# Grouped output stores of an expert layer: 16 KB and 8 KB rows in place of 4 KB rows

## The chip, the cores and the metric

The kernel runs on one core of a Trainium2 chip. The metric is the device time of one execution in microseconds (us), as the median of several runs. The core has a matrix engine (PE), a vector engine (DVE), a scalar engine (ACT), GpSimd (POOL), a sync engine (SP), and sixteen DMA engines that move data between HBM and the on-chip memory SBUF. Matmul results land in PSUM, from where DVE or ACT copies them to SBUF ("eviction"). SBUF and PSUM have 128 partitions.

## The reference

Eight experts each apply a two-layer network to their own 256 tokens:

```python
# x [8, 256, 512], w1 [8, 512, 2048], w2 [8, 2048, 512], b1 [8, 2048], b2 [8, 512], all float32
h = np.matmul(x, w1) + b1[:, np.newaxis, :]
h = np.maximum(h, 0)
return (np.matmul(h, w2) + b2[:, np.newaxis, :]).astype(np.float32)   # [8, 256, 512]
```

The weights are 64 MB of float32 (67.1 million bytes), each used once. The result is 4 MB, 512 KB per expert.

## The kernel before

The weights are loaded by GpSimd's DMA queue, which casts them to fp16 on the way. One expert has 2 MB of w1 and 2 MB of w2 as fp16. The program runs in steps: step s does the first product of expert s and the second product of expert s - 3 (LAG = 3). Buffers for w1 and w2 are three each, so a load is issued when an older expert's matmuls have released a buffer.

```python
LAG = 3
LATE = range(E - 2)                       # experts 0 to 5
PARTS = {E - 2: ((0, 25, False), (25, 121, True), (121, 128, False))}
w1_pool = ctx.enter_context(tc.tile_pool(name="w1", bufs=3))
w2_pool = ctx.enter_context(tc.tile_pool(name="w2", bufs=3))
hT_pool = ctx.enter_context(tc.tile_pool(name="hT", bufs=LAG + 1))
out_pool = ctx.enter_context(tc.tile_pool(name="outp", bufs=E))
psum_h = ...bufs=3        # first product, [128, 256] float32 each
psum_o = ...bufs=2        # second product, two tiles of [128, 512] float32 each

def first_product(e):
    hT[e] = hT_pool.tile([P, nJ, T], fp16, tag="hT", name="hT")
    for j in range(nJ):                                   # 16 blocks of hidden units
        ph = psum_h.tile([P, T], fp32, tag="ph", name="ph")
        for kc in range(nKC):                             # 4 matmuls, ph = [hidden unit, token]
            ordered(nc.tensor.matmul(out=ph, lhsT=w1_sb[e]..., rhs=xT[e][:, kc, :], ...))
        nc.scalar.activation(out=hT[e][:, j, :], in_=ph, func=Relu, bias=b1T[...], scale=1.0)
        if j == nJ // 2 and e + 1 < E:
            transposes(e + 1)

def flush(e):
    dst, src = pending.pop(e)
    ordered(nc.gpsimd.dma_start(out=dst, in_=src))

def store(e, po):
    out_sb = out_pool.tile([P, nTB, H], fp32, tag="out", name="out")
    nc.vector.tensor_copy(out=out_sb[:, 0, :], in_=po[0])
    nc.scalar.copy(out=out_sb[:, 1, :], in_=po[1])
    dst = out[e].rearrange("(p tb) h -> p tb h", tb=nTB)  # a partition holds two result rows, 4 KB
    if e in LATE:
        pending[e] = (dst, out_sb)
        return
    for p0, p1, scalar in PARTS.get(e, ((0, P, False),)):
        (nc.scalar if scalar else nc.sync).dma_start(out=dst[p0:p1], in_=out_sb[p0:p1])

def second_product(e):
    ...   # bias row by a matmul with ones, then 16 matmuls for each half tb of the tokens:
    #       po[tb] += hT[e][:, j, tb * P : (tb + 1) * P] (transposed) x w2_sb[e][:, j, :]
    store(e, po)

# the ring holds loads and then the flushes; it is served from the front, in order
for e in LATE:
    ring.append((e + LAG + 1, flush, (e,)))
for s in range(E + LAG):
    while ring and ring[0][0] <= s:
        _, put, args = ring.pop(0)
        put(*args)
    if s < E:
        first_product(s)
    if s >= LAG:
        second_product(s - LAG)
```

Within each block of 256 tokens, the transposes put the tokens in such a column order that column tb * 128 + p is token 2p + tb. So partition p of the two result tiles holds rows 2p and 2p + 1, which lie side by side in HBM. The flushes of experts 0 to 5 stand in GpSimd's queue behind all loads. Expert 6 is stored in three pieces from SP and ACT, expert 7 in one from SP.

Of the kernel before, what the change touches and what calls it, by code (L numbers as in the profile page):

```python
# [10 lines left out]
def kernel(  # L11
# [9 lines left out]
    nc = tc.nc  # L21
    fp32 = mybir.dt.float32
    fp16 = mybir.dt.float16
    E, T, H = x.shape
    M = w1.shape[2]
    P = 128
    nTB = T // P
# [4 lines left out]
    LAG = 3  # L32

    LATE = range(E - 2)


    PARTS = {E - 2: ((0, 25, False), (25, 121, True), (121, 128, False))}
# [3 lines left out]
    def ordered(ins):  # L43
        return tc.keep_in_program_order(ins)
# [4 lines left out]
    x_pool = ctx.enter_context(tc.tile_pool(name="xp", bufs=1))  # L49
    xT_pool = ctx.enter_context(tc.tile_pool(name="xTp", bufs=2))  # L50
    hT_pool = ctx.enter_context(tc.tile_pool(name="hT", bufs=LAG + 1))
    out_pool = ctx.enter_context(tc.tile_pool(name="outp", bufs=E))
    psum_h = ctx.enter_context(tc.tile_pool(name="psum_h", bufs=3, space=bass.MemoryType.PSUM))
    psum_o = ctx.enter_context(tc.tile_pool(name="psum_o", bufs=2, space=bass.MemoryType.PSUM))

# [8 lines left out]
    w2_sb = [None] * E  # L64
    hT = [None] * E
    pending = {}

    def load_x(first, n):

        R = n * T // P  # L70
        t = x_pool.tile([P, R, H], fp16, tag=f"x{first}", name=f"x{first}")
        ordered(nc.gpsimd.dma_start(  # L72
            out=t, in_=x[first : first + n].rearrange("e (p r) h -> (e p) r h", r=R)
        ))
        for i in range(n):
            x16[first + i] = (t, i * (P // n), R)
# [13 lines left out]
    def transposes(e):  # L90


        t, p0, R = x16[e]
        n = R // nTB
        xT[e] = xT_pool.tile([P, nKC, T], fp16, tag="xT", name="xT")
        for g in range(T // R // B):
            src = t[p0 + B * g : p0 + B * (g + 1)]
            for b in range(nB):
                block = src[:, :, b * (H // nB) : (b + 1) * (H // nB)].rearrange(
                    "p (n tb) (i kc) -> p tb kc n i", tb=nTB, kc=nKC)  # L100
                out = xT[e][b * B : (b + 1) * B].rearrange(
                    "p kc (tb g i n) -> p tb g kc n i", tb=nTB, i=B, n=n)
                if n == 1:
                    nc.vector.transpose(out=out[:, :, g, :, 0, :], in_=block[:, :, :, 0, :])  # L104
                    continue
                for tb in range(nTB):
                    nc.vector.transpose(out=out[:, tb, g], in_=block[:, tb])  # L107

    def first_product(e):
        hT[e] = hT_pool.tile([P, nJ, T], fp16, tag="hT", name="hT")  # L110
        for j in range(nJ):
            bias_at = j * B + e * nB + nB - 1
            ph = psum_h.tile([P, T], fp32, tag="ph", name="ph")
            for kc in range(nKC):
                ordered(nc.tensor.matmul(  # L115
                    out=ph,
                    lhsT=w1_sb[e][:, kc, :].rearrange("p (q j) -> p q j", j=nJ)[:, :, j],
                    rhs=xT[e][:, kc, :],
                    start=(kc == 0),
                    stop=(kc == nKC - 1),  # L120
                ))
            nc.scalar.activation(  # L122
                out=hT[e][:, j, :],
                in_=ph,
                func=mybir.ActivationFunctionType.Relu,
                bias=b1T[:, bias_at : bias_at + 1],
                scale=1.0,
            )
            if j == nJ // 2 and e + 1 < E:
                transposes(e + 1)  # L130

    def flush(e):
        dst, src = pending.pop(e)
        ordered(nc.gpsimd.dma_start(out=dst, in_=src))  # L134

    def store(e, po):
        out_sb = out_pool.tile([P, nTB, H], fp32, tag="out", name="out")
        nc.vector.tensor_copy(out=out_sb[:, 0, :], in_=po[0])  # L138
        nc.scalar.copy(out=out_sb[:, 1, :], in_=po[1])  # L139
        dst = out[e].rearrange("(p tb) h -> p tb h", tb=nTB)  # L140
        if e in LATE:
            pending[e] = (dst, out_sb)
            return
        for p0, p1, scalar in PARTS.get(e, ((0, P, False),)):
            (nc.scalar if scalar else nc.sync).dma_start(out=dst[p0:p1], in_=out_sb[p0:p1])

    def second_product(e):
        po = []
        for tb in range(nTB):
            t = psum_o.tile([P, H], fp32, tag=f"po{tb}", name=f"po{tb}")  # L150
            po.append(t)
            ordered(nc.tensor.matmul(  # L152
                out=t, lhsT=ones1, rhs=b2_sb[0:1, e * H : (e + 1) * H], start=True, stop=False,
            ))
        half = nJ // 2 if e == E - 1 else nJ
        for lo in range(0, nJ, half):
            for tb in range(nTB):
                for j in range(lo, lo + half):
                    ordered(nc.tensor.matmul(  # L159
                        out=po[tb],  # L160
                        lhsT=hT[e][:, j, tb * P : (tb + 1) * P],
                        rhs=w2_sb[e][:, j, :],
                        start=False,
                        stop=(j == nJ - 1),
                    ))
        store(e, po)

    x32 = []
    for e in range(nXF32):
# [4 lines left out]
        out=b2_sb,  # L174
        in_=b2.rearrange("e h -> (e h)").rearrange("(o f) -> o f", o=1),
# [12 lines left out]
    for b in range(nB):  # L188
        nc.vector.transpose(  # L189
            out=b1T[b * B : (b + 1) * B, nB - 1 - b : nB - 1 - b + nJ * B],  # L190
            in_=b1_rows.rearrange("r (i j) -> r j i", j=nJ),
# [4 lines left out]
    ring = []  # L196
# [5 lines left out]
        if s >= LAG:  # L202
            ring.append((s - 2, load_w2, (s - LAG,)))
    ring.append((E + LAG - 3, load_w2, (E - 1, ((0, nJ // 2), (nJ // 2, nJ)))))
    for e in LATE:
        ring.append((e + LAG + 1, flush, (e,)))

    for s in range(E + LAG):
        while ring and ring[0][0] <= s:
# [6 lines that stand above are left out]
# [31 lines left out]
```

## Time and profile before

| | before |
|---|---|
| median of 3 runs | 182.35 us (182.2 to 182.7) |
| span of the profiled execution | 180.0 us |
| PE, DVE, ACT busy | 130.3, 78.1, 62.5 us |
| mean granted PE clock | 0.938 |
| DMA packets | 4260, 40.56 MB |
| w1 load, 2048 KB, issue to landing | 33.6 us |
| store of one expert by GpSimd, 512 KB, issue to landing | 22.7 us |
| store of expert 7 by SP, 512 KB, issue to landing | 4.4 us |

The profile has a page with the busy time of each engine, the span in 40 slices (a digit is the busy share in tenths), the DMA queues and groups of instructions. Further views list instructions in order of time, or cut the span into stretches. In a group, L122 is line 122 of the kernel, "x128" the number of instructions, and the mean time of one is in nanoseconds. A DMA's "issue to landing" includes the time that it stands in its queue behind earlier ones. The trace also keeps each DMA packet's queue, size and duration.

### The profile page before, as it was taken

To read this page: it belongs to the slowest core of one execution; us is meant where nothing else is said; L and a number is where in the kernel's file an instruction comes from. 1 tells how busy PE (TensorE), PEld (TensorE's weight loads), DVE (VectorE), ACT (ScalarE), POOL (GpSimd) and SP (SyncE) were. 2 spreads that over 40 slices of the span, in tenths; PEclk is the share of its full clock that TensorE was granted. 3 is DMA by queue.
4 is the path that set the end of the run, shared out by engine and by line. 5 is a ranking of instruction groups with operands and counts; after the bars stand their busy time and mean duration, and the time that the engine had idled before them with its cause. 6 is when DMAs were issued, how large, how long until landed. Compare 5 with 4: busy or idle time off the path is not lost.

```text
span 180.0 us, 1937 instructions
## 1 busy us (share of the span) xinstructions
PE 130.3 (72%) x784; PEld 87.4 (49%) x784; DVE 78.1 (43%) x111; ACT 62.5 (35%) x137; POOL 15.0 (8%) x31
## 2 busy tenths in 40 slices
PE   0006199999398950899769994959796899959960
PEld 0004079998286410794359543934395343324420
DVE  1999931988000099999990697000000010101010
ACT  0000558999177010491137403930186001100110
POOL 7100000220201010001100001000100008010000
PEclk9999999999879996599988999987999699999998
DMA  6999999998999999899999999999998999899996
GB/s 207 259 226 198 233 200 208 233 231 182 231 229 193 218 233 226 186 229 229 211 200 233 226 193 222 229 215 197 233 229 189 222 229 226 186 215 209 330 421 246
DMA packets 4260, 40.56 MB, mean 225 GB/s; under 512 B 508, under 2 KB 524, under 8 KB 1948
## 3 DMA queue, kind: packets, MB, share of 16 engines
q0 software_dynamic: 3664, 38.35, 96.5%
q1 hardware_dynamic: 476, 1.70, 2.6%
q10 hardware_dynamic: 112, 0.39, 0.5%
q8 instruction: 6, 0.10, 0.2%
q14 instruction: 2, 0.02, 0.0%
HBM read 71.39 MB, written 4.19 MB: 420 GB/s over the span
## 4 chain that ended last, share of the span: by engine, by line
DMA 44%; PE 30%; another core or an unknown queue 11%; DVE 9%; ACT 1%; issue 1%; POOL 0%; POOLq 0%; ACTq 0%
DMA w1sb<-in_w_dram 26%; PE ph L115 18%; DMA w2sb<-in_w_dram 17%; PE po L159 12%; DVE xT L104 6%; DVE b1T L189 2%; DMA x<-in_x_dram 2%; DVE x L182 1%; ACT L122 1%; PE po L152 1%; ACT out L139 0%; POOL w2sb L88 0%; ACT hT L122 0%; POOLq L88 0%
## 5 line engine op out<-in xcount | busy, mean ns | idle before, releaser
L115 PE MATMUL ph<-xT,w1sb 128*128 128x256 f16 x512 | 66.4, 298 | 36.2 <-DMA w1sb<-in_w_dram 24.9
L115 PEld LDWEIGHTS <-w1sb 128*128 128x128 f16 x512 | 60.9, 148 | 42.5 <-DMA w1sb<-in_w_dram 34.3
L107 DVE STREAM_TRANSPOSE xT<-x 32x256 f16<-32x256 f16 (+1 forms) x64 | 53.0, 888 | 31.9 <-DMA x<-in_x_dram 18.2
L159 PE MATMUL po<-w2sb,hT 128*128 128x512 f16 x256 | 59.7, 393 | 7.6 <-DMA w2sb<-in_w_dram 7.5
L122 ACT ACTIVATE hT<-ph,b1T 128x256 f16<-128x256 f32 x128 | 56.5, 474 | 24.6 <-PE ph L115 24.5
L159 PEld LDWEIGHTS <-hT 128*128 128x128 f16 x256 | 25.6, 100 | 41.6 <-issue 14.9
L138 DVE COPY out<-po 128x512 f32<-128x512 f32 x8 | 5.5, 692 | 58.3 <-PE po L159 58.2
L139 ACT COPY out<-po 128x512 f32<-128x512 f32 x8 | 4.7, 586 | 67.3 <-PE po L159 67.3
L104 DVE STREAM_TRANSPOSE xT<-x 32x256 f16<-32x256 f16 x32 | 13.9, 436 | 0.5
L88 POOL DMA_DIRECT2D w2sb<-in_w_dram x9 | 4.8, 532 | 73.3 <-PE po L159 73.3
L80 POOL DMA_DIRECT2D w1sb<-in_w_dram x8 | 4.9, 609 | 64.7 <-PE ph L115 63.9
L122 ACT ACT_TABLE_LOAD x1 | 1.3, 1283 | 20.2 <-DVE b1T L189 20.2
L152 PE MATMUL po<-b_sb,ones 1*128 1x512 f16 x16 | 4.8, 379 | 0.0
L189 DVE STREAM_TRANSPOSE b1T<-b_rows 32x512 f32<-32x512 f32 x4 | 4.1, 1037 | 0.1
L134 POOL DMA_DIRECT2D out_dram<-out x6 | 3.2, 536 | 7.2 <-DMA w2sb<-in_w_dram 7.2
L182 DVE CAST x<-x 128x1024 f16<-128x1024 f32 x2 | 1.4, 693 | 3.2 <-DMA x<-in_x_dram 3.2
L152 PEld LDWEIGHTS <-ones 1*128 1x128 f16 x16 | 0.9, 92 | 2.1 <-issue 2.1
L72 POOL DMA_DIRECT2D x<-in_x_dram x2 | 1.1, 554 | 0.0
L178 DVE MEMSET ones<- 1x128 f16 x1 | 0.2, 165 | 0.8 <-PEq L231 0.8
L177 POOL DMA_DIRECT2D b_rows<-in_b_dram x1 | 0.5, 515 | 0.0
L173 POOL DMA_DIRECT2D b_sb<-in_b_dram x1 | 0.5, 511 | 0.0
L231 POOL MEMSET const-float32-0.0<- 128x1 f32 x1 | 0.1, 99 | 0.2 <-issue 0.2
(3 smaller groups left out, 0.3 us busy)
## 6 DMA issues: line engine op xcount, KB each, us to landing
w1sb<-in_w_dram POOLq DMA_DIRECT2D x8, 2048.0 KB, 33.6
w2sb<-in_w_dram POOLq DMA_DIRECT2D x7, 2048.0 KB, 43.2
out_dram<-out POOLq DMA_DIRECT2D x6, 512.0 KB, 22.7
w2sb<-in_w_dram POOLq DMA_DIRECT2D x2, 1024.0 KB, 17.4
x<-in_x_dram SPq DMA_DIRECT2D x2, 512.0 KB, 3.8
x<-in_x_dram POOLq DMA_DIRECT2D x1, 1024.0 KB, 30.3
x<-in_x_dram POOLq DMA_DIRECT2D x1, 512.0 KB, 24.0
out_dram<-out SPq DMA_DIRECT2D x1, 512.0 KB, 4.4
```

What stands on the lines that cost most here:

```text
L80: ordered(nc.gpsimd.dma_start(out=w1_sb[e], in_=w1[e].rearrange("(p kc) m -> p kc m", kc=nKC)))
L88: ordered(nc.gpsimd.dma_start(out=w2_sb[e][:, lo:hi], in_=src[:, lo:hi]))
L104: nc.vector.transpose(out=out[:, :, g, :, 0, :], in_=block[:, :, :, 0, :])
L107: nc.vector.transpose(out=out[:, tb, g], in_=block[:, tb])
L115: ordered(nc.tensor.matmul(out=ph, lhsT=w1_sb[e][:, kc, :].rearrange("p (q j) -> p q j", j=nJ)[:, :, j], rhs=xT[e][:, kc, :], start=(kc == 0),
L122: nc.scalar.activation(out=hT[e][:, j, :], in_=ph, func=mybir.ActivationFunctionType.Relu, bias=b1T[:, bias_at : bias_at + 1], scale=1.0,)
L134: ordered(nc.gpsimd.dma_start(out=dst, in_=src))
L138: nc.vector.tensor_copy(out=out_sb[:, 0, :], in_=po[0])
L139: nc.scalar.copy(out=out_sb[:, 1, :], in_=po[1])
L152: ordered(nc.tensor.matmul(out=t, lhsT=ones1, rhs=b2_sb[0:1, e * H : (e + 1) * H], start=True, stop=False,))
L159: ordered(nc.tensor.matmul(out=po[tb], lhsT=hT[e][:, j, tb * P : (tb + 1) * P], rhs=w2_sb[e][:, j, :], start=False, stop=(j == nJ - 1),))
L189: nc.vector.transpose(out=b1T[b * B : (b + 1) * B, nB - 1 - b : nB - 1 - b + nJ * B], in_=b1_rows.rearrange("r (i j) -> r j i", j=nJ),)
```

## The change

The results of experts 0 to 3 are gathered in one SBUF tile of 128 partitions x 16 KB, and those of experts 4 and 5 in one of 128 partitions x 8 KB. Each tile is stored by one DMA from GpSimd, so a partition's contiguous run in HBM is 16 KB or 8 KB instead of 4 KB. The purpose is fewer and longer DMA packets and fewer DMAs.

For a group of four, expert e's rows must lie in 32 partitions, eight result rows in each. Result rows come out of PE one per partition, so the tokens must be reordered. That is done in the eviction of the first product: ACT reads the PSUM columns with a step of 4 elements (2 in the group of two) and writes hT in runs of 32 (64) columns. Each result tile then holds, in each run of 32 partitions, rows that belong to one place of the eight. The copies out of PSUM are cut accordingly: four of 32 partitions in place of one of 128 (two of 64 in the group of two), and each writes to the partitions of its expert. Experts 6 and 7 stay as they were.

```diff
--- before.py
+++ after.py
@@ -33,7 +33,7 @@
 
 
 
-    LATE = range(E - 2)
+    GROUPS = {0: 4, 4: 2}
 
 
     PARTS = {E - 2: ((0, 25, False), (25, 121, True), (121, 128, False))}
@@ -49,7 +49,8 @@
     x_pool = ctx.enter_context(tc.tile_pool(name="xp", bufs=1))
     xT_pool = ctx.enter_context(tc.tile_pool(name="xTp", bufs=2))
     hT_pool = ctx.enter_context(tc.tile_pool(name="hT", bufs=LAG + 1))
-    out_pool = ctx.enter_context(tc.tile_pool(name="outp", bufs=E))
+    group_pool = ctx.enter_context(tc.tile_pool(name="groups", bufs=1))
+    out_pool = ctx.enter_context(tc.tile_pool(name="outp", bufs=2))
     psum_h = ctx.enter_context(tc.tile_pool(name="psum_h", bufs=3, space=bass.MemoryType.PSUM))
     psum_o = ctx.enter_context(tc.tile_pool(name="psum_o", bufs=2, space=bass.MemoryType.PSUM))
 
@@ -64,6 +65,8 @@
     w2_sb = [None] * E
     hT = [None] * E
     pending = {}
+    results = {}
+    group_of = {first + i: (first, n) for first, n in GROUPS.items() for i in range(n)}
 
     def load_x(first, n):
 
@@ -108,6 +111,7 @@
 
     def first_product(e):
         hT[e] = hT_pool.tile([P, nJ, T], fp16, tag="hT", name="hT")
+        split = group_of[e][1] if e in group_of else 1
         for j in range(nJ):
             bias_at = j * B + e * nB + nB - 1
             ph = psum_h.tile([P, T], fp32, tag="ph", name="ph")
@@ -120,8 +124,8 @@
                     stop=(kc == nKC - 1),
                 ))
             nc.scalar.activation(
-                out=hT[e][:, j, :],
-                in_=ph,
+                out=hT[e][:, j, :].rearrange("p (tb k i) -> p tb k i", tb=nTB, k=split),
+                in_=ph.rearrange("p (tb i k) -> p tb k i", tb=nTB, k=split),
                 func=mybir.ActivationFunctionType.Relu,
                 bias=b1T[:, bias_at : bias_at + 1],
                 scale=1.0,
@@ -129,17 +133,30 @@
             if j == nJ // 2 and e + 1 < E:
                 transposes(e + 1)
 
-    def flush(e):
-        dst, src = pending.pop(e)
+    def flush(first):
+        dst, src = pending.pop(first)
         ordered(nc.gpsimd.dma_start(out=dst, in_=src))
 
     def store(e, po):
-        out_sb = out_pool.tile([P, nTB, H], fp32, tag="out", name="out")
-        nc.vector.tensor_copy(out=out_sb[:, 0, :], in_=po[0])
-        nc.scalar.copy(out=out_sb[:, 1, :], in_=po[1])
-        dst = out[e].rearrange("(p tb) h -> p tb h", tb=nTB)
-        if e in LATE:
-            pending[e] = (dst, out_sb)
+        if e in group_of:
+            first, n = group_of[e]
+            split, rows = n, P // n
+            if e == first:
+                results[e] = group_pool.tile(
+                    [P, split * nTB, H], fp32, tag=f"out{e}", name=f"out{e}")
+        else:
+            first, n, split, rows = e, 1, 1, P
+            results[e] = out_pool.tile([P, nTB, H], fp32, tag="out", name="out")
+        out_sb = results[first]
+        at = (e - first) * rows
+        for k in range(split):
+            part = slice(k * rows, (k + 1) * rows)
+            nc.vector.tensor_copy(out=out_sb[at : at + rows, k * nTB, :], in_=po[0][part])
+            nc.scalar.copy(out=out_sb[at : at + rows, k * nTB + 1, :], in_=po[1][part])
+        dst = out[first : first + n].rearrange("e (p r) h -> (e p) r h", r=split * nTB)
+        if e in group_of:
+            if e == first + n - 1:
+                pending[first] = (dst, out_sb)
             return
         for p0, p1, scalar in PARTS.get(e, ((0, P, False),)):
             (nc.scalar if scalar else nc.sync).dma_start(out=dst[p0:p1], in_=out_sb[p0:p1])
@@ -202,8 +219,8 @@
         if s >= LAG:
             ring.append((s - 2, load_w2, (s - LAG,)))
     ring.append((E + LAG - 3, load_w2, (E - 1, ((0, nJ // 2), (nJ // 2, nJ)))))
-    for e in LATE:
-        ring.append((e + LAG + 1, flush, (e,)))
+    for first, n in GROUPS.items():
+        ring.append((first + n + LAG, flush, (first,)))
 
     for s in range(E + LAG):
         while ring and ring[0][0] <= s:
```

## The prediction

> **What bounds the kernel now.** I read three views in this order: the slices of the page, the kinds of DMA queue, and the table of stretches of time; then the timeline of GpSimd (POOL) and of the end, to see how much room each issue leaves.
>
> The slices and the queues of the page first:
>
> ```profile
> DMA  6999999998999999899999999999998999899996
> ...
> q0 software_dynamic: 3664, 38.35, 96.5%
> q1 hardware_dynamic: 476, 1.70, 2.6%
> q10 hardware_dynamic: 112, 0.39, 0.5%
> ...
> HBM read 71.39 MB, written 4.19 MB: 420 GB/s over the span
> ```
>
> The sixteen DMA engines are busy in every slice, and the packets of the three data queues together take 96.5 + 2.6 + 0.5 = 99.6% of sixteen engines' span. No compute engine is near that (PE is busy 72%, ACT 35%). So the span is set by the amount of DMA work, as long as the queue never runs dry. The stretches say the same (start and end; busy time of the engines with instruction counts; granted clock; DMA share; GB/s written):
>
> ```profile
> 15.00:60.00 45.00, 36.71 (x267) 32.23 (x268) 21.83 (x48) 29.58 (x65) 4.23 (x8) 0.96 1.00 213
> 60.00:100.00 40.00, 30.04 (x185) 20.95 (x184) 31.49 (x26) 14.50 (x32) 1.58 (x3) 0.87 1.03 219
> 100.00:140.00 40.00, 32.05 (x204) 21.16 (x202) 11.40 (x10) 16.06 (x37) 1.05 (x2) 0.96 1.01 216
> 140.00:168.00 28.00, 25.47 (x107) 10.49 (x107) 2.08 (x3) 1.76 (x3) 4.20 (x8) 0.94 1.00 211
> 168.00:174.00 6.00, 6.00 (x28) 2.52 (x26) 0.69 (x1) 0.00 (x0) 0.00 (x0) 1.00 1.02 410
> 174.00:178.00 4.00, 0.00 (x1) 0.00 (x0) 0.00 (x0) 0.59 (x1) 0.00 (x0) 1.00 0.98 401
> 178.00:180.00 2.00, 0.00 (x0) 0.00 (x0) 0.00 (x0) 0.00 (x0) 0.00 (x0) 0.55 0.15 59
> ```
>
> Up to 168 us the queue carries loads (about 215 GB/s written as fp16 is 430 GB/s read as fp32), from 168 to 178 the stores at 401 to 410 GB/s, with a DMA share of 0.98 or more throughout. All six stores that the change touches lie in that last part: they sit in the same queue behind the last weights.
>
> The timeline shows why the order of the end matters (start, length, instruction, what ended the idle time before):
>
> ```profile
> 149.03 1.06 POOL L88 DMA_DIRECT2D w2sb<-in_w_dram  x2 [19.05 <-PE po L159]
> 150.07 2.63 POOL L134 DMA_DIRECT2D out_dram<-out  x5
> ...
> 159.92 0.53 POOL L134 DMA_DIRECT2D out_dram<-out  x1 [7.22 <-DMA w2sb<-in_w_dram]
> ...
> 166.92 7.08 PE L159 MATMUL po<-w2sb,hT 128*128 128x512 f16 x32
> ...
> 174.04 0.59 ACT L139 COPY out<-po 128x512 f32<-128x512 f32 x1 [6.96 <-PE po L159]
> ```
>
> Five stores are issued at 150 and one at 159.9, but the packet records of the trace put their first packet at 168.1 us, after the last weight packet on that engine, and their last at 178.0. Expert 7's result is only ready at 174.6; its store's packets run from about 176.5 to 179.3. So the end has two bounds close together: DMA work, and the matmuls of expert 7 plus one store.
>
> [...] the last store's packets, on SyncE's queue, begin while the six stores' packets are still being served, and go on after their end at 178.0. [...] no instruction of the kernel before reads PSUM with a stride. [...]
>
> **The change part by part.**
>
> *Stores: six of 512 KB become one of 2 MB and one of 1 MB.* The bytes stay 3 MB. The packets go from 6 x 128 of 4 KB to 128 of 16 KB and 128 of 8 KB. I size them from the weight loads. Successive 2 MB loads land 9.686 us apart: 8 rows per engine, 1,210.7 ns per row that reads 32 KB. The first half of the last w2 lands 4.867 us after the transfer before it: 608.4 ns per row of 16 KB read. The difference, 602.3 ns per 16 KB, is 27.2 bytes/ns per engine; 6 ns per packet are fixed. A store packet of 4 KB is followed by the next after 155.3 ns: 4,096 / 27.2 = 150.6, so 4.7 ns fixed. Then a 16 KB packet costs about 602.3 + 4.7 = 607.0 against 4 x 155.3 = 621.2: 14.2 ns saved per row, 8 rows per engine, 0.114 us. An 8 KB packet saves one fixed part: 4.7 x 8 = 0.038 us. Four completion writes fewer at about 6 ns: 0.023 us. Together 0.17 us of DMA work at the end, on the bounding resource. Expert 7's store cannot use more than its own delay: after the six stores it still has 179.3 - 178.0 = 1.3 us of packets, so it stays last and simply moves forward by those 0.17 us.
>
> *Issue.* The two new issues wait for older landings and for the copies of expert 3 and expert 5. The compiled order has GpSimd wait for one old transfer before the first and for none before the second, so the 7.22 us wait of the sixth store goes. It is worth nothing: the queue is full of weights until 168. Four issues of 0.53 us also go, in a place where GpSimd is idle.
>
> *Copies out of PSUM.* Per expert 0 to 3 one DVE copy of 692 ns and one ACT copy of 586 ns become four each on 32 partitions, for experts 4 and 5 two each on 64. The free size stays 512, so I give each the same time: 3 x 0.59 = 1.8 us more ACT and 3 x 0.69 = 2.1 us more DVE per expert, ACT in all 14 x 0.586 = 8.2 us, DVE 14 x 0.692 = 9.7 us. ACT's extra 1.8 us comes just before evictions of a first product, which has three PSUM buffers. PE may stall there about 1 us, less where it was waiting for a load anyway (36.2 us of idle before those matmuls).
>
> *Column order in the evictions.* For experts 0 to 3 each of 64 ACT evictions reads PSUM with a step of 16 bytes, for 4 and 5 each of 32 with 8 bytes; the count and element count are unchanged. I expect 474 ns to stay. The matmuls read hT contiguously as before.
>
> *Does any of this let the queue run dry?* What counts is how long before the queue would have been empty each load is issued. The first gated load, w1 of expert 3, is issued at 31.08 when PE has done expert 0; the load before it lands at 37.35, so 6.3 us to spare. The next ones, at 38.06 and 45.05, have 24 us or more, those from 57 to 89 some 39 to 45. Towards the end the room shrinks: w2 of expert 5 at 108.59 has 31.6, of expert 6 at 129.45 has 20.4, of expert 7 at 149.03 has 10.5 (the queue then holds work until 159.56). The last three are released by matmuls that themselves wait for a landed w2. A stall of 1 us at the start of a first product does not reach the queue.
>
> The sum: -0.17 us on the DMA path, +0 from all else. 182.35 - 0.17 = 182.18; I say 182.15.
>
> **The rivals.**
>
> First, slow strided evictions. [...] To dry the queue it would have to add over 0.39 us per eviction[...]. Against it: ACT is idle 65% of the span and the later loads have far more room. In favour: DVE's transposes of 512 elements with 8-byte steps take 1,328 ns against 448 for 256, more than twice[...].
>
> Second, long packets delay the last store. [...] But both sets must be done before the end, and their sum does not change. It costs nothing unless an engine idles.
>
> Third, larger gain. If long rows made HBM writes faster than the slope found from loads, up to 1.3 us could come before expert 7's packets alone set the end: 176.5 plus eight packets of 0.155 is 177.7, against 179.3. Against it: 4 KB store packets already run at 150.6/155.3 = 97% of the load slope.
>
> Fourth, an uneven share of the sixteen engines. The last completions of the final store spread from 177.8 to 179.3. If the larger packets fell unevenly the last engine would be later by one of them, 0.3 to 0.6 us. Against: 128 rows are 8 per engine, before and after.
>
> **Range and chances.** The three times of the kernel before spread over 0.5 us, more than the 0.17 that I expect. The range of 181.5 to 182.8 takes in that spread, half of the third rival and the fourth. A 2% step is 3.6 us. Faster by that is out of reach, as DMA work of 178 us stays[...]. Chances: faster 0.01, same 0.975, slower 0.015.
>
> **What would show it.** After the change the DMA digits should stay at 9 throughout and q0's share near 96.5%. The store packets should take about 610 and 310 ns; the last w2 should land at 169.4 as before, and the six experts' stores end near 177.8 instead of 178.0. The ACT group of L122's successor should stay at 474 ns; 32-partition copies at 586 and 692 ns. The prediction is wrong if the DMA line has a gap near 37 us, if evictions take over 0.85 us, if the long packets run at another rate than 27 bytes/ns, or if expert 7's store lands more than 0.5 us earlier or later than 4.4 us after its issue.

## The result, and the profile after

The changed kernel takes 181.72 us (median of six runs, 181.52 to 182.0) against 182.34 us before: a ratio of 0.9965 with a 95% interval of 0.995 to 0.9981. A second set, with 13 executions against 34 of the kernel before, gave 181.77 against 182.16 us, a ratio of 0.9972 (0.9962 to 0.9983); I had expected 0.9965 if the first gain of 0.62 us held, and 0.999 if only the 0.17 us of DMA work was saved. The gain is clear of the noise, 0.4 to 0.6 us by the medians, and well below 2%.

First the page of the changed kernel (slices, queues, bytes):

```profile
DMA  5999998999999999999999999999999999999995
...
q0 software_dynamic: 3088, 38.35, 96.3%
q1 hardware_dynamic: 476, 1.70, 2.5%
q10 hardware_dynamic: 112, 0.39, 0.5%
...
HBM read 71.39 MB, written 4.19 MB: 420 GB/s over the span
```

The bytes are the same, q0 has 576 packets fewer (3664 - 3088), and the DMA engines are still busy in every slice. There is no gap near 37 us: up to the last weights the queue never ran dry. So a difference inside the span has to be looked for in its last stretches (start and end; busy time of PE, weight loads, DVE, ACT, POOL; granted clock; DMA share; GB/s):

```profile
140.00:168.00 28.00, 25.21 (x100) 10.19 (x99) 3.45 (x5) 2.32 (x4) 2.12 (x4) 0.89 1.01 215
168.00:174.00 6.00, 6.00 (x29) 2.58 (x29) 0.02 (x1) 0.58 (x1) 0.00 (x0) 1.00 0.98 412
174.00:178.00 4.00, 1.67 (x8) 0.58 (x6) 0.67 (x1) 0.59 (x1) 0.00 (x0) 1.00 0.86 354
178.00:180.00 2.00, 0.00 (x0) 0.00 (x0) 0.00 (x0) 0.00 (x0) 0.00 (x0) 1.00 0.22 86
```

From 174 to 178 the DMA share is 0.86 where it was 0.98. Cut finer, the gap lies after 176 (the changed kernel, then the kernel before):

```profile
176.00:178.00 2.00, 0.00 (x0) 0.00 (x0) 0.00 (x0) 0.29 (x1) 0.00 (x0) 1.00 0.71 291
176.00:178.00 2.00, 0.00 (x0) 0.00 (x0) 0.00 (x0) 0.00 (x0) 0.00 (x0) 1.00 0.96 391
```

Some DMA engines have stored their share of the six results, and expert 7's is not yet there. The timeline says why:

```profile
149.78 0.54 POOL L138 DMA_DIRECT2D out_dram<-out  x1
...
158.19 0.54 POOL L138 DMA_DIRECT2D out_dram<-out  x1 [7.87 <-ACT out L155]
159.37 8.75 PE L176 MATMUL po<-w2sb,hT 128*128 128x512 f16 x32 [2.14 <-DMA w2sb<-in_w_dram]
...
168.59 7.08 PE L176 MATMUL po<-w2sb,hT 128*128 128x512 f16 x32
...
175.70 0.59 ACT L155 COPY out<-po 128x512 f32<-128x512 f32 x1 [6.96 <-PE po L176]
```

Expert 6's 32 matmuls take 8.75 us where the same stretch took 7.07 in the profile of before. The granted clock is at half (0.50) for 3.4 us from 159.9 on; its mean from 159 to 168 us is 0.81, against 1.00 before. So expert 7's result is ready at 176.3 instead of 174.6, and its store then needs 2.6 us from issue to landing instead of 4.4. The span is still 0.15 us shorter (179.83 against 179.98).

The packet records show how both can be true. Before, the sixteen DMA engines end expert 7's store one after another, between 177.3 and 178.7 us, and the last one sets the end. In the changed kernel engines run out of packets from about 176 on, but the last of them ends the group of two at 177.17, as expert 7's first packets start, and all sixteen end between 178.45 and 178.60. So the late result fell into time in which most engines had slack and the last one had none. One profile each can't say how much this matters; the experiments below do.

Last, the groups that the change touches (engine, operation, form, count; busy us, mean ns):

```profile
L126 ACT ACTIVATE hT<-ph,b1T 128x256 f16<-128x256 f32 x128 | 56.2, 473 | 13.8 <-PE ph L119 13.7
...
L154 DVE COPY out<-po 32x512 f32<-32x512 f32 x16 | 11.0, 687 | 12.8 <-PE po L176 12.6
L155 ACT COPY out<-po 32x512 f32<-32x512 f32 x16 | 9.2, 577 | 37.3 <-PE po L176 37.2
```

The evictions take 473 ns with 96 of the 128 reading PSUM in steps, against 474 with none. A copy from 32 partitions costs about as much as one from 128 (577 and 687 ns against 586 and 692 before).

### The profile page after: what moved, and what is told of

Its sections match the earlier page's. It is cut to its first block, busy times and chain, and to the rows that moved or that the text cites. A ratio compares the mean times of both kernels' runs of the same rounds, so it can differ in the third digit from the quotient of the medians.

```text
span 179.8 us, 1957 instructions
## 1 busy us (share of the span) xinstructions
PE 131.3 (73%) x784; PEld 86.7 (48%) x784; DVE 87.8 (49%) x125; ACT 70.2 (39%) x151; POOL 12.9 (7%) x27
## 3 DMA queue, kind: packets, MB, share of 16 engines
q0 software_dynamic: 3088, 38.35, 96.3%
## 4 chain that ended last, share of the span: by engine, by line
DMA 57%; PE 23%; DVE 13%; issue 2%; ACT 1%; POOL 0%; DVEq 0%; ACTq 0%
DMA w2sb<-in_w_dram 39%; DMA x<-in_x_dram 19%; PE po L176 13%; PE ph L119 10%; DVE xT L107 6%; DVE xT L110 5%; DVE b1T L206 2%; DVE x L199 1%; ACT L126 1%; PE po L169 1%; ACT out L155 0%; POOL w1sb L83 0%; ACT hT L126 0%; POOL w2sb L91 0%; DVEq L110 0%
## 5 line engine op out<-in xcount | busy, mean ns | idle before, releaser
L119 PE MATMUL ph<-xT,w1sb 128*128 128x256 f16 x512 | 64.2, 291 | 34.2 <-DMA w1sb<-in_w_dram 24.0
L119 PEld LDWEIGHTS <-w1sb 128*128 128x128 f16 x512 | 59.3, 147 | 39.8 <-DMA w1sb<-in_w_dram 32.5
L176 PE MATMUL po<-w2sb,hT 128*128 128x512 f16 x256 | 63.1, 409 | 10.2 <-DMA w2sb<-in_w_dram 10.2
L176 PEld LDWEIGHTS <-hT 128*128 128x128 f16 x256 | 26.5, 104 | 46.6 <-issue 22.1
L154 DVE COPY out<-po 32x512 f32<-32x512 f32 (+2 forms) x22 | 15.1, 688 | 56.4 <-PE po L176 56.2
L155 ACT COPY out<-po 32x512 f32<-32x512 f32 (+2 forms) x22 | 12.7, 578 | 72.2 <-PE po L176 72.0
L138 POOL DMA_DIRECT2D out_dram<-out x2 | 1.1, 540 | 7.9 <-ACT out L155 7.9
```

Source lines behind the costliest of these rows:

```text
L119: ordered(nc.tensor.matmul(out=ph, lhsT=w1_sb[e][:, kc, :].rearrange("p (q j) -> p q j", j=nJ)[:, :, j], rhs=xT[e][:, kc, :], start=(kc == 0),
L154: nc.vector.tensor_copy(out=out_sb[at : at + rows, k * nTB, :], in_=po[0][part])
L155: nc.scalar.copy(out=out_sb[at : at + rows, k * nTB + 1, :], in_=po[1][part])
L176: ordered(nc.tensor.matmul(out=po[tb], lhsT=hT[e][:, j, tb * P : (tb + 1) * P], rhs=w2_sb[e][:, j, :], start=False, stop=(j == nJ - 1),))
```

## The experiments

The kernel before ran beside each set on the same chip, so ratios are to it. A ratio is on record with its interval and need not be the quotient of the medians given. The experiment on the kernel before itself shows the noise. In the edits, "..." stands for lines left out.

**The kernel before again.** No edit.

> The kernel before once more, unchanged, so that the spread of its own runs and spans is known. Every theory: ratio to the kernel before 1.000 within 0.002, span about 180.0. If the half-clock stretch of PE near the end (the last two second products take 7.1 us each at full clock, 8.75 with a half-clock stretch) falls differently from run to run, the runs spread over some 0.5 us and the profile may show expert 7's store issued near 176.3 instead of 174.6.

Ratio 1.0016 (0.9997 to 1.0035), median 182.31. Two of its 14 executions took 183.4 and 184.41 us, more than any other of this kernel, so a single execution can stray by 2 us with nothing changed. Its profile has a half-clock stretch at the end, as the changed kernel's had: the last matmul starts at 175.1 us, where it was 173.6 in the first profile of the same kernel, and expert 7's store lands in 3.3 us. The position of that stretch is therefore not a property of the change.

**The compute part alone, and the two halves of the store part.** Three kernels take the change apart. The first is the kernel before with:

```diff
-                out=hT[e][:, j, :],
-                in_=ph,
+                out=hT[e][:, j, :].rearrange("p (tb k i) -> p tb k i", tb=nTB, k=split),
+                in_=ph.rearrange("p (tb i k) -> p tb k i", tb=nTB, k=split),
...
-        nc.vector.tensor_copy(out=out_sb[:, 0, :], in_=po[0])
-        nc.scalar.copy(out=out_sb[:, 1, :], in_=po[1])
+        for k in range(split):
+            part = slice(k * P // split, (k + 1) * P // split)
+            nc.vector.tensor_copy(out=out_sb[part, 0, :], in_=po[0][part])
+            nc.scalar.copy(out=out_sb[part, 1, :], in_=po[1][part])
```

> The kernel before with the strided evictions and the split copies only, six stores of 4 KB rows as before (the rows of a result come out in another order). My prediction: no cost, no gain, ratio 1.000, because PE waits for loads. Theory that the gain is in the compute part (other phase of PE, other landing of the half-clock stretches): ratio 0.9965. Theory that the compute part costs something that the stores hide: 1.001 to 1.003.

Ratio 1.0003 (0.9993 to 1.0014). The strided evictions and 28 more copies cost nothing that can be measured, and bring nothing.

The second is the changed kernel with padding, which keeps two DMAs but cuts their packets to 4 KB:

```diff
-                    [P, split * nTB, H], fp32, tag=f"out{e}", name=f"out{e}")
+                    [P, split, nTB * H + PAD], fp32, tag=f"out{e}", name=f"out{e}")
...
-                pending[first] = (dst, out_sb)
+                pending[first] = (dst, out_sb[:, :, 0 : nTB * H])
```

> The changed kernel, but the group tiles are padded by 64 bytes after each 4 KB, so the two DMAs move 4 KB packets: two DMAs, short rows. Theory of row length: the gain goes, ratio to before 1.000, 768 packets of 159 ns. Theory of the number of DMAs: the gain stays, ratio 0.9965. If the compute part alone brings it, 0.9965 too, and the run with the compute part alone tells the two apart.

Ratio 0.9993 (0.9982 to 1.0004), median 182.08. Most of the gain is gone without the long rows. But something remains that the span does not show, and it led to the next step: see the table below.

The third keeps the long rows and gives each expert its own DMA, out of the 32 (or 64) partitions that hold its rows:

```diff
-            if e == first + n - 1:
-                pending[first] = (dst, out_sb)
+            pending[e] = (dst[at : at + rows], out_sb[at : at + rows])
...
+    for e in range(E - 2):
+        ring.append((e + LAG + 1, flush, (e,)))
```

> The changed kernel, but each of experts 0 to 5 is stored by its own DMA from 32 partitions of 16 KB (64 of 8 KB for experts 4 and 5): long rows, six DMAs. Theory of row length: all of the gain stays, ratio to before 0.9965 within 0.0015, about 181.7 us. Theory of the number of DMAs (completions, issues, what is done after the last one): the gain goes, ratio 1.000. The sum of my prediction (0.15 us for packets, 0.02 for completions) would put it at 182.2 against 182.34.

Ratio 1.0256 (1.0214 to 1.0298), median 186.44: slower by 4.2 us, which no theory had. Its profile in stretches (columns as above):

```profile
168.00:174.00 6.00, 6.00 (x29) 2.55 (x26) 0.69 (x1) 0.00 (x0) 0.00 (x0) 1.00 1.01 328
174.00:178.00 4.00, 0.05 (x1) 0.00 (x0) 0.00 (x0) 0.58 (x1) 0.00 (x0) 0.82 0.95 299
178.00:180.00 2.00, 0.00 (x0) 0.00 (x0) 0.00 (x0) 0.00 (x0) 0.00 (x0) 0.50 0.91 285
180.00:182.00 2.00, 0.00 (x0) 0.00 (x0) 0.00 (x0) 0.00 (x0) 0.00 (x0) 0.50 0.46 172
```

The DMA share stays at 0.91 or more until 180, yet the rate falls to 328 GB/s and then below 300, where the changed kernel had 412 from 168 to 174. The engines are occupied, and their packets take longer: in the packet records the first 64 of the 128 packets of 16 KB, two experts' worth, take 611 to 624 ns; the other 64 take 993 ns on average and up to 2,182. The slowing begins at 170.4 us, before the packets of expert 6's store start at 170.9. The two experts that went first lie in partitions 0 to 63, the two with the slow packets in 64 to 127. No run here shows what slows them, and the cause of the loss stays open.

The same six DMAs and 27 DMAs of GpSimd in all, but each from 128 partitions with 4 KB per partition:

```diff
-        ordered(nc.gpsimd.dma_start(out=dst, in_=src))
+        pieces = {0: 4, 4: 2}[first]
+        step = GROUPS[first] * nTB // pieces
+        for i in range(pieces):
+            cut = slice(i * step, (i + 1) * step)
+            ordered(nc.gpsimd.dma_start(out=dst[:, cut], in_=src[:, cut]))
```

> The changed kernel, but each group tile is stored in pieces of 4 KB per partition, all from 128 partitions: four DMAs for experts 0 to 3, two for 4 and 5. So six DMAs and 4 KB packets as before, with 27 DMAs of GpSimd. If time minus span hangs on the count of DMAs: 2.03 us. Inside the span the long rows' saving of 0.17 us is gone: a mean span near 180.2 as the kernel before; together 182.2, ratio 1.000. If the long rows from 32 partitions cost 4.2 us because of the 32 partitions and not because there are six DMAs, this kernel shows no such loss.

Ratio 0.9995 (0.9983 to 1.0007), median 182.04: no loss. Six DMAs as such do no harm here. Long rows as such do none either, as the changed kernel stores them from 128 partitions (181.77 us). Long rows from 32 and 64 partitions do (186.44 us); short rows from so few were not tried. That is why the change stores a whole group by one DMA, and not each expert as soon as its long rows are there.

**Is the end bound by DMA work or by PE?** Two kernels are meant to keep PE from the half-clock stretch, by matmuls in the wait before expert 6's second product whose result nobody reads:

```diff
+        if e == E - 2:
+            warm = psum_h.tile([P, T], fp32, tag="ph", name="warm")
+            for i in range(WARM):                      # WARM = 20
+                ordered(nc.tensor.matmul(
+                    out=warm, lhsT=hT[e - 1][:, i % nJ, 0:P], rhs=w2_sb[e - 1][:, i % nJ, 0:T],
+                    start=(i == 0), stop=(i == WARM - 1)))
```

> The changed kernel with 20 matmuls more, whose result nobody reads, in the 2.1 us in which PE waits for w2 of expert 6, so that no half-clock stretch falls into the last two second products. Theory that the end is then bound by DMA work alone: expert 7 ready at 174.6 in every run, the end set by the stores; the time falls by up to 0.3 us against the changed kernel, and its runs spread less. Theory that PE does not matter for the end: no difference from the changed kernel.

> The same 20 matmuls in the kernel before. With PE out of the way in both, the difference between this run and the changed kernel with the same matmuls is the DMA work alone: 0.17 us by my packet sum (ratio of the two 0.999), 0.6 us or more if long rows save more than their packets show. Against the kernel before: 1.000, as its end is bound by DMA work already when PE is at full clock.

The changed kernel with it: ratio 0.9978 (0.9968 to 0.9988), 181.83 us. The kernel before with it: 1.0002 (0.999 to 1.0014), 182.35 us. In the timeline of the first the stretch is absent, and the granted clock is 1.00 from 159 to 176 us:

```profile
157.43 2.36 PE L176 MATMUL warm<-w2sb,hT 128*128 128x256 f16 x20
...
159.64 7.07 PE L183 MATMUL po<-w2sb,hT 128*128 128x512 f16 x32
...
174.29 0.59 ACT L156 COPY out<-po 128x512 f32<-128x512 f32 x1 [6.96 <-PE po L183]
```

Expert 7's result is ready at 174.9 instead of 176.3, and the time does not fall: 181.83 against 181.77 without it in the same set. So the half-clock stretch is not what ends either kernel, as far as these executions show, and the gain of the change (181.83 against 182.35, 0.5 us) is not a matter of PE. The expected 0.3 us against the changed kernel did not come. Nor is the 0.5 us all DMA work, as the second expectation had it: the mean spans of the two differ by 0.24 us, and the rest lies outside the span, as the table below shows.

How near PE's bound lies, the kernel before shows without the six stores. It leaves the results of experts 0 to 5 in SBUF:

```diff
-    for e in LATE:
-        ring.append((e + LAG + 1, flush, (e,)))
```

> The kernel before without the six stores of experts 0 to 5 (their results stay in SBUF; only experts 6 and 7 are stored). It shows where the matmuls of the end alone would put the time. With 6 x 1.25 = 7.5 us of DMA work gone, the end is expert 7's matmuls and its own store: ready at 174.6 (176.3 with a half-clock stretch of PE), then about 3.8 us as for the 512 KB loads at the start, so a span of 178.5 to 180.1 instead of 180.0 to 180.4. If the two bounds lie so close, the time falls by only 0.3 to 1.5 us, ratio 0.992 to 0.998. If the end were bound by DMA work alone, it would fall by far more, 4 us or so.

Ratio 0.9906 (0.9873 to 0.994), median 180.1: more than the 0.3 to 1.5 us expected. Expert 7's store took 2.6 us from issue to landing and not the 3.8 assumed. Four of its six spans are 178.1 to 178.5, two are 179.7 and 179.8. Its profiled execution, with a span of 178.1:

```profile
168.00:174.00 6.00, 5.91 (x28) 2.45 (x26) 0.69 (x1) 0.06 (x1) 0.00 (x0) 1.00 0.25 81
174.00:178.00 4.00, 0.00 (x0) 0.00 (x0) 0.00 (x0) 0.53 (x1) 0.00 (x0) 1.00 0.32 131
```

DMA is idle three quarters of the time from 168 to 174, and the time still falls by 2 us only, not by the 4 or so of an end bound by DMA work alone: 7.5 us of DMA work taken away meet expert 7's matmuls and its own store. The two longer spans fit a half-clock stretch, which costs 1.68 us (8.75 - 7.07), but those executions were not looked into. So the bounds at the end are a span of 178.1 us (or 179.7) by PE and of 180.2 by DMA work.

**What lies outside the span.** The runs list the time and the span of every execution. Means over the executions, worked out from these lists (GpSimd DMAs counted over the whole kernel). One execution of the kernel before with PE kept busy, of 233.5 us at a granted clock of 0.605 where the others have 0.94 or so, is left out:

| kernel | GpSimd DMAs | store rows | mean span (executions) | time minus span |
|---|---|---|---|---|
| before, in the three sets | 27 | 4 KB | 180.17 (35), 180.19 (34), 180.19 (59) | 2.03 to 2.04 |
| before again | 27 | 4 KB | 180.48 (14) | 2.03 |
| compute part alone | 27 | 4 KB | 180.19 (14) | 2.03 |
| before, PE kept busy | 27 | 4 KB | 180.30 (13) | 2.03 |
| six stores by columns | 27 | 4 KB | 180.09 (14) | 2.03 |
| six stores from 32 or 64 partitions | 27 | 16, 8 KB | 184.80 (6) | 2.03 |
| three stores | 24 | 8 KB | 180.19 (21) | 1.78 |
| two padded stores | 23 | 4 KB | 180.33 (14) | 1.79 |
| changed kernel, first set and again | 23 | 16, 8 KB | 179.97 (6), 180.02 (13) | 1.79, 1.78 |
| changed, PE kept busy | 23 | 16, 8 KB | 180.06 (14) | 1.78 |
| changed, four memsets | 23 | 16, 8 KB | 180.00 (22) | 1.78 |
| changed, expert 6 in one store | 23 | 16, 8 KB | 180.33 (13) | 1.78 |
| without the six stores | 21 | none | 178.73 (6) | 1.78 |

The gain has two parts. Inside the span it is 180.19 - 180.02 = 0.17 us, and 0.19 with the memset kernel. Outside it is 2.03 - 1.78 = 0.25 us. Together they make up the 0.43 and 0.44 us by which the mean times of the two larger sets differ. Two of the kernels were made to find what the second part hangs on.

```diff
+    spare = [singles.tile([1, 128], fp32, name=f"spare{i}") for i in range(4)]
...
+        for i in range(2):
+            ordered(nc.gpsimd.memset(spare[first // 4 * 2 + i], 0.0))
         ordered(nc.gpsimd.dma_start(out=dst, in_=src))
```

> The changed kernel with four one-partition memsets of 128 elements on GpSimd ahead of its two stores, where GpSimd is idle; it then has as many GpSimd instructions as the kernel before, but 23 DMAs of GpSimd and not 27. So far the time minus the span is 2.03 us in every kernel with six GpSimd stores and 1.78 us in those with two or none. If that 0.25 us hangs on the count of GpSimd instructions: time minus span 2.03, median near 182.0. If it hangs on the count of DMAs: 1.78, median near 181.8.

Ratio 0.998 (0.9973 to 0.9987), median 181.75, time minus span 1.78: not the number of GpSimd instructions.

```diff
+        pieces = {0: 2, 4: 1}[first]                     # the rest as in the kernel by columns
```

> The changed kernel with the first group stored in two DMAs of 8 KB rows: 24 DMAs of GpSimd, three of them stores. If time minus span goes in proportion to the DMAs (0.25 us for four): 1.84 us. If it is a step somewhere between 23 and 27: 1.78 or 2.03. Inside the span, 0.08 us less is saved by rows of 8 KB than by 16 KB: median 181.85 to 182.1.

Ratio 0.9986 (0.9975 to 0.9997), median 182.0, time minus span 1.78: not in proportion to the DMAs, but a step between 24 and 27. Together with the six stores by columns (2.03 in the changed kernel's own layout), the count of GpSimd's DMAs is what goes with it. All these kernels issue the same 21 loads from GpSimd, so the count of all its DMAs can't be told from the count of its stores (six against three, two or none). Whether the 0.25 us are spent ahead of the first instruction or after the last, and what does it, was not seen.

**The uneven pieces of expert 6.**

```diff
-    PARTS = {E - 2: ((0, 25, False), (25, 121, True), (121, 128, False))}
+    PARTS = {E - 2: ((0, 128, True),)}
```

> The changed kernel with expert 6's result stored in one DMA of 128 partitions from ACT, not in three of 25, 96 and 7 partitions. Two DMAs fewer on the hardware queues. If the uneven pieces make some DMA engines end later, the last completions lie closer together and the time falls by up to 0.3 us (5 rows more of 0.155 us on some engines would be 0.78 us); if the pieces even out engines that lag, it rises by as much. If the DMAs of SP count for the time outside the span as those of GpSimd might, time minus span falls below 1.78.

Ratio 0.9991 (0.9978 to 1.0003), median 182.19, mean span 180.33, time minus span still 1.78. It gives back 0.3 us of the span, so the uneven pieces seem to help the changed kernel as they stand; how they do was not looked into. DMAs of the hardware queues do not enter the time outside the span, as far as two of them tell. No kernel tried beats the changed one.

## Why the prediction was right, and what it lacked

- *The kernel is bound by DMA work to the end; the queue never runs dry.* Right up to the last weights: the first gated load, w1 of expert 3, is issued at 30.45 us, and the load ahead of it lands at 38.49. At the end it holds for the engine that ends last, not for all sixteen (share 0.71 from 176 to 178). Neither PE at full clock (ratio 1.0002 for the kernel before, 181.83 against 181.77 us for the changed one) nor the compute part alone (1.0003) moves the time.
- *Packets.* Right. Predicted were 607.0 ns per row of 16 KB from the spacing of weight loads. In the changed kernel successive 16 KB packets start 607 ns apart on an engine (168.186, 168.793, 169.400 us), and 8 KB packets 306 apart, where 4 KB packets before start 155.3 apart; with eight rows of each length on an engine that saves 0.15 us. The records give 611 and 309 ns per packet for the predicted 610 and 310.
- *0.17 us saved on the DMA path.* In the two profiles the last w2 lands at 169.22 before and 169.21 after, and the last of the six results at 177.84 and 177.62. The mean spans differ by 0.17 to 0.19 us. Both agree. But kernels whose GpSimd stores all move 4 KB packets range from 180.09 to 180.33 us (the two padded stores), leaving aside the set with the two stray executions, so the size is confirmed to some 0.1 us and no better. The three stores, at 180.19 where 180.1 was expected, show the same scatter or a small cost that was not followed up.
- *Packet times.* The times that the prediction takes from the packet records stand 0.54 us later than the clock of its timelines. On that clock the six stores' packets run from 167.54 to 177.48 us and expert 7's from 176.0 to 178.7, and the first gated load has 5.7 us to spare, not 6.3. The differences between packets, on which the sum rests, are not touched.
- *Evictions, copies, issue: nothing.* Right. The first rival, slow strided evictions, is out: 473 against 474 ns. PE's wait for evictions is 4.1 us in all, against 4.0.
- *Long packets delay the last store (second rival).* Not seen. Where expert 7's store is issued while the DMA engines are still full, in the changed kernel with PE kept busy (share 1.01 from 174 to 176 us, result ready at 174.9), it lands 4.5 us after its issue; in the kernel before with PE kept busy, 4.7.
- *A larger gain (third rival).* Larger by 0.25 to 0.45 us, but not for its reason: the rate of long rows is that of the loads (16 KB stored in 607 ns, against 608.4 for a load's row of 16 KB).
- *An uneven share of the engines (fourth rival).* The last engine is no later for the longer packets: expert 7's store lands at 178.94 us, against 179.08. But the end does hang on the last engine, and the size of expert 6's pieces moved the span by 0.3 us.
- *The sum, -0.17 + 0.* This is the step that fell short. The term for four issues and completions fewer was 0.023 us, all inside the span. It put a completion at 6 ns, which was an estimate: the pages count 64 packets under 512 B fewer (508 - 444), sixteen for each DMA, and in the packet records of before GpSimd's 4-byte packets take 10.9 ns on average from 166 us on. The runs showed 0.25 us more, outside it. The time was taken as the span plus a constant; the constant depends on the kernel. No term of the prediction stood for this. The range of 181.5 to 182.8 took the result in because of the spread of 0.5 us and the third rival that it allowed for, which is luck as far as the 0.25 us go.
- *Expert 7's store lands 4.4 us after its issue.* Wrong: 2.6 us, after an issue 1.7 us later, which is beyond the 0.5 us that the prediction named as a sign of being wrong. The half-clock stretch was not foreseen, and the store needs less time when the queue is empty: 2.6 us also without the six stores. The end hardly moves because the two effects offset each other.

## What to carry to other kernels

When the DMA engines are full from start to end, size a change of row length from the spacing of packets that the trace already has: fixed part per packet times packets per engine. Here 4 KB rows already ran at 97% of the rate, so rows four times as long could give only tenths of a microsecond. Gather results so that long rows still come from all 128 partitions (here 611 ns a packet, against up to 2,182 from 32), and look at the engine that ends last, and at the time minus the span as well as the span, before putting a small difference down to the transfers.

## What was not expected of the hardware

- Time minus span is 2.03 us with 27 DMAs from GpSimd, six of them stores, and 1.78 with 24 or fewer, three or fewer of them stores, to 0.01 us in the mean of every kernel. Counts between were not run.
- 2 MB stored in 16 KB rows ran at 611 ns a packet from 128 partitions, but in four DMAs of 32 partitions with packets of up to 2,182 ns; with them, and with the other two experts stored from 64 partitions, the kernel took 4.2 us longer.
- After a wait of PE of 2.13 us the next 32 matmuls took 7.07 us in one execution, at a granted clock of 1.00; after one of 2.14 us they took 8.75 us in another, at 0.80. The half-clock stretches that the trace of the changed kernel holds whole last 3.4 or 6.8 us. What sets one off was not shown.
- ScalarE read PSUM with steps of 8 and 16 bytes as fast as without (473 against 474 ns).
